# Split weights that start at multiples of 128 bytes, with the x tiles left 32 bytes beyond one, in a float32 decoder layer

## The chip, the cores and the metric

The kernel runs on one core of a Trainium2 chip. The metric is the device time of one execution in microseconds. Three runs of the kernel before gave a median of 1759.82 us (1758.56 to 1761.3). On one core work these engines: TensorE (PE, with its weight loads shown as PEld), VectorE (DVE), ScalarE (ACT), GpSimd (POOL) and SyncE (SP). Each has its own queue of instructions and takes them in order; POOL and SP issue most of the DMAs. Between the engines only semaphores keep order. Operands lie in SBUF, 128 partitions with 229,376 bytes each in the layout of this program; the sums of products lie in PSUM.

## The reference

One layer of a decoder, for 256 rows (S) of 2048 channels (D), in float32:

```python
x = x + 0.5 * swiglu(rmsnorm(x, ffn1_norm[l]), ffn1_w_gate[l], ffn1_w_up[l], ffn1_w_down[l])
h = rmsnorm(x, mix_norm[l])
a_q, a_k, a_v, m_q, m_k, m_v, m_o, m_i, m_f = jnp.split(h @ w_in[l], split_idx, axis=-1)
...
x = x + jnp.concatenate([y_a, y_b], axis=-1) @ w_out[l]
x = x + 0.5 * swiglu(rmsnorm(x, ffn2_norm[l]), ffn2_w_gate[l], ffn2_w_up[l], ffn2_w_down[l])
...
return rmsnorm(x, final_norm)
```

`y_a` is a causal differential attention with 4 heads, `y_b` an mLSTM with 4 heads in chunks of 128 rows. The inner width of each FFN is 5632. Nearly all the arithmetic is in the seven weight matrices of the two FFNs and the two projections, some 50 million weights that are read once.

## The kernel before

**Products.** TensorE multiplies float32r operands. To keep float32 accuracy, each weight and each x is split into a high part (`split`, L132: a cast on ScalarE, `wh` or `xs`/`xt`) and a low part (L133: a subtraction on VectorE, `wl`). `mms` (L177 to L184) then makes three matmuls of each product: L181 high x by high w, L182 low x by high w, L184 high x by low w. The x tile, 128x128, is the stationary operand; the weights, up to 512 columns of float32r, are the moving one. So each 512-column matmul reads 2048 bytes of `wh` or `wl` in every partition.

**Stages.** The kernel runs FFN1, the input projection with the mLSTM gates and the attention beside it, the output projection, and FFN2, in column chunks (`CW` = 512; the q/k part has chunks of 392, 384 and 256). The class `Paired` works two weight matrices or two halves at a time in a scheme that saves products at the price of sums of weights on VectorE (L479, L497) and by accumulating DMAs on POOL (L495, L533); its steps are `leading`, `second_sum` and `sums`. `sums` copies two banks of PSUM to SBUF through ScalarE (`ds` and `us`, L503, called from `sums`) and subtracts them on VectorE (L537, L546). `units` and `plain` do the remaining rows without that scheme.

**Residual and norm.** After a chunk of an FFN or of the output projection, `residual` (or `finish2` for the last FFN, L1211 and L1213) adds it to `xres`, and `square_sum` (L298 to L300) squares the new 512 columns on ScalarE. Only the sum of the squares (`accum_out`) is used; the squares themselves go to a tile called `junk`.

**Order.** The kernel writes no fixed order for the engines: a planner orders each engine's queue when the program is built, by priorities (`tc.high_priority`, with `AHEAD` and `soon`), by when buffers come free, and by a few explicit orders (`after`, `ahead_of_splits`). A tile pool with n buffers gives its tiles out in turn, and a tile waits until the one that held the buffer is done. So a tile that comes from another pool can change the order that the planner finds.

**SBUF.** Pools take their space one behind the other in the order in which they are opened. Before, with the start of the tiles in bytes modulo 128:

| Pool (buffers) | Tiles | First byte | Modulo 128 |
|---|---|---|---|
| const, big | `prm`, `ident` and others; `xres` | 16512; `ident` 16928; `xres` 20256 | `ident` 32; `xres` 32 |
| slots (22) | `xs`, `xt`, 4096 bytes | 36640 | 32 |
| work (8) | ring of 512-column tiles, tag "w" | 126752 | 32, 64, 96, 0 in turn |
| wr (5) | `raw`, 6144 bytes | 143392 | 32 |
| wrp (5) | `rawp`, `late`, 4096 bytes | 174112 | 32 |
| wsp (4 + 4) | `wh` and `wl`, 4096 bytes | 194592 and 210976 | 32 |
| small | sums and scales, `junk` | 227360 | mixed |

The ring tiles of `work` take 2080 bytes each, which is why they rotate. SBUF is full but for 32 bytes. The ring holds `ds`, `us`, `sg`, `xg`, `hg`, `xsum` and `part`, among others.

Of the kernel before, what the change touches and what calls it, by code (L numbers as in the profile page):

```python
# [9 lines left out]
F32 = mybir.dt.float32  # L10
F32R = mybir.dt.float32r
BF16 = mybir.dt.bfloat16
AF = mybir.ActivationFunctionType
# [4 lines left out]
P = 128  # L18
# [6 lines left out]
CW = 512  # L25
# [35 lines left out]
def tile_trunk_layer(ctx: ExitStack, tc: tile.TileContext, x, xt, par, bias_if, lamv, fnorm,  # L61
                     wg1, wu1, wd1, wqk0, wqk1, wqk2, win, wout, wg2, wu2, wd2, out):
    nc = tc.nc
    const = ctx.enter_context(tc.tile_pool(name="const", bufs=1))
    big = ctx.enter_context(tc.tile_pool(name="big", bufs=1))
    slots = ctx.enter_context(tc.tile_pool(name="slots", bufs=22))
    work = ctx.enter_context(tc.tile_pool(name="work", bufs=8))
    wr = ctx.enter_context(tc.tile_pool(name="wr", bufs=5))
    wrp = ctx.enter_context(tc.tile_pool(name="wrp", bufs=5))
    wsp = ctx.enter_context(tc.tile_pool(name="wsp", bufs=4))  # L70
    small = ctx.enter_context(tc.tile_pool(name="small", bufs=2))
    ps_acc = ctx.enter_context(tc.tile_pool(name="ps_acc", bufs=4, space=PSUM))
    ps_tr = ctx.enter_context(tc.tile_pool(name="ps_tr", bufs=2, space=PSUM))

    wqk = [wqk0, wqk1, wqk2]
    uid = [0]

    def nm(s):
        uid[0] += 1
        return f"{s}_{uid[0]}"  # L80


    prm = const.tile([P, N_PAR], F32, name="prm")
    nc.scalar.dma_start(prm, par)
    zeros = work.tile([P, CW], BF16, tag="w", name="zeros")
# [13 lines left out]
        nc.tensor.matmul(seeded(which), zeros[:, 0:P], zeros, start=True, stop=True)  # L99
    for _ in range(WARM):  # L100
        nc.tensor.matmul(warm, zeros[:, 0:P], zeros, start=True, stop=True)
    ident = const.tile([P, P], F32, name="ident")
    nc.gpsimd.memset(ident, 0.0)
    nc.gpsimd.affine_select(out=ident, in_=ident, compare_op=ALU.not_equal, fill=1.0, base=0,
                            pattern=[[-1, P]], channel_multiplier=1)
# [190 lines left out]
        return r  # L296

    def square_sum(src, acc, scale=1.0):  # L298
        j = small.tile([P, CW], BF16, tag="junk", name=nm("junk"), bufs=1)
        nc.scalar.activation(j[:, 0:src.shape[-1]], src, AF.Square, scale=scale, accum_out=acc)  # L300

    def finish_norm(parts):
        tot = small.tile([P, NT], F32, tag="tot", name=nm("tot"))
# [57 lines left out]
    def residual(accs, c, scale, parts):  # L361
        for hb in range(NT):
            add_half(accs[hb], xres[:, hb, c * CW:(c + 1) * CW], scale)
        for hb in range(NT):
            square_sum(xres[:, hb, c * CW:(c + 1) * CW], parts[:, hb, c:c + 1])
# [19 lines left out]
    def wk(name):  # L385
        return work.tile([P, CW], F32, tag="w", name=nm(name))
# [652 lines left out]
    for hb in range(NT):  # L1039
        for h in range(NH):  # L1040
            i = hb * NH + h
            square_sum(hms[hb][:, h, :], ssm[:, i:i + 1], scale=dd[:, i:i + 1])
# [68 lines left out]
    def weighted(h):  # L1111
        ps = ps_acc.tile([P, NT, VD], F32, tag="acc", name=nm("av"))
        vs = [av[h // 2][:, hb, h % 2 * VD:(h % 2 + 1) * VD] for hb in range(NT)]
        nc.tensor.matmul(ps[:, 0, :], wts[h][:, 0:P], vs[0], start=True, stop=True)
        nc.tensor.matmul(ps[:, 1, :], wts[h][:, P:S], vs[0], start=True, stop=False)
        nc.tensor.matmul(ps[:, 1, :], wts[h][:, S:S + P], vs[1], start=False, stop=True)
        ss = small.tile([P, NT], F32, tag="ssa", name=nm("ssa"))
        for hb in range(NT):
            square_sum(ps[:, hb, :], ss[:, hb:hb + 1])
        ra = rsq(ss, NT, float(VD), "ra")  # L1120
        y = mixt([P, NT, VD], name="ya")
        for hb in range(NT):
            vec.tensor_scalar(y[:, hb, :], ps[:, hb, :], ra[:, hb:hb + 1], None, op0=ALU.mult)
        if h == 0:
            side.append(lambda: None)
        side.append(functools.partial(y_transposes, [y[:, hb, :] for hb in range(NT)], 2 * h, gatt))
# [141 lines left out]
```

## Time and profile before

| | |
|---|---|
| Median of three runs | 1759.82 us |
| The profiled execution | 1759.56 us |
| Its span, first to last instruction | 1757.8 us |
| Mean granted TensorE clock | 0.999 |
| HBM read / written | 349.56 MB / 2.10 MB |
| TensorE matmuls in the trace | 7926 |

The profile was taken from one execution. "Busy" counts instructions that do work. A matmul's listed duration runs from its start to the end of its results and overlaps the next ones, so that the rate of matmuls is read from the distance between their starts. In a group of instructions the numbers after the bar are the busy time, the mean duration of one in ns, and the idle time of the engine just before them with what ended it.

### The profile page before, as it was taken

What the parts mean: (1) busy time and instruction counts of PE and PEld (TensorE: products, weight loads), DVE (VectorE), ACT (ScalarE), POOL (GpSimd) and SP (SyncE); (2) the same over time, 40 slices, a digit from 0 to 9 for tenths busy, and PEclk for the clock granted to TensorE, in tenths of its full rate; (3) what the DMA queues carried; (4) which work ended last, traced back from release to release, by engine and by line L of the source; (5) the groups of instructions that cost most, each with busy time, mean ns of one, the idle gap of its engine ahead of it and who ended that gap; (6) DMA issues with size and microseconds to landing.
All of it is one profiled execution on the core that took longest, in us unless ns stands there. A gap on an engine that the chain in (4) does not pass through costs nothing.

```text
span 1757.8 us, 24486 instructions
## 1 busy us (share of the span) xinstructions
PE 1744.6 (99%) x7926; PEld 1437.7 (82%) x7926; DVE 1617.8 (92%) x2189; ACT 1267.4 (72%) x1949; POOL 429.3 (24%) x630
## 2 busy tenths in 40 slices
PE   9999999999999999999999999999999999999998
PEld 7788888888888888987888888888888878888886
DVE  7999999999999999898888999999999999999997
ACT  8666777777677768777687777776777677677765
POOL 0022332322233312012231101122332332233310
PEclk9999999999999999999999999999999999999999
DMA  9787998999799977577886667898998999799973
GB/s 365 251 254 209 259 261 265 253 292 265 218 262 258 263 252 204 185 230 221 236 238 192 209 210 211 260 265 233 258 260 268 241 268 276 232 246 256 283 254 115
DMA packets 155265, 429.72 MB, mean 244 GB/s; under 512 B 17632, under 2 KB 18944, under 8 KB 154880
## 3 DMA queue, kind: packets, MB, share of 16 engines
q0 software_dynamic: 76304, 196.66, 45.1%
q1 hardware_dynamic: 77680, 229.40, 38.0%
q10 hardware_dynamic: 1152, 2.09, 0.3%
q8 instruction: 62, 1.02, 0.2%
q14 instruction: 67, 0.55, 0.1%
HBM read 349.56 MB, written 2.10 MB: 200 GB/s over the span
## 4 chain that ended last, share of the span: by engine, by line
PE 93%; DMA 2%; DVE 2%; issue 1%; ACT 0%; POOL 0%; SPq 0%; POOLq 0%; DVEq 0%; ACTq 0%
PE acc L184 18%; PE acc L181 18%; PE acc L182 18%; PE accn L181 12%; PE accn L182 12%; PE accn L184 12%; DVE wl L133 1%; DMA raw<-in_wg_dram 1%; PE tr L373 1%; DMA raw<-in_wu_dram 1%; PE tr L314 0%; PE sc L1060 0%; DMA rawp<-in_wg_dram 0%; ACT wh L132 0%; PE num L1011 0%
## 5 line engine op out<-in xcount | busy, mean ns | idle before, releaser
L132 ACT CAST wh<-raw 128x512 fp32r<-128x512 f32 (+2 forms) x885 | 601.5, 708 | 214.5 <-PE acc L182 66.3
L133 DVE TENSOR_TENSOR wl<-raw,wh 128x512 fp32r<-128x512 f32 (+2 forms) x885 | 676.1, 793 | 58.4 <-ACT wh L132 54.5
L132 ACT CAST wh<-rawp 128x1024 fp32r<-128x1024 f32 (+3 forms) x308 | 318.2, 1035 | 109.5 <-PE acc L182 55.1
L133 DVE TENSOR_TENSOR wl<-rawp,wh 128x1024 fp32r<-128x1024 f32 (+3 forms) x308 | 367.1, 1197 | 32.0 <-ACT wh L132 29.8
L181 PE MATMUL acc<-wh,xs 128*128 128x512 f32 (+2 forms) x956 | 369.5, 387 | 0.0
L182 PE MATMUL acc<-wh,xs 128*128 128x512 f32 (+2 forms) x956 | 368.9, 386 | 0.0
L184 PE MATMUL acc<-wl,xs 128*128 128x512 f32 (+2 forms) x956 | 317.6, 387 | 0.8 <-DVE wl L133 0.7
L533 POOL DMA_DIRECT2D raw<-late x176 | 152.6, 1053 | 442.7 <-DVE wl L133 422.9
L181 PE MATMUL acc<-wh,xt 128*128 128x512 f32 (+2 forms) x564 | 218.4, 388 | 0.7 <-ACT wh L132 0.7
L182 PE MATMUL acc<-wh,xt 128*128 128x512 f32 (+2 forms) x564 | 217.3, 386 | 0.0
L181 PE MATMUL accn<-wh,xt 128*128 128x512 f32 (+1 forms) x552 | 215.3, 391 | 0.0
L182 PE MATMUL accn<-wh,xt 128*128 128x512 f32 (+1 forms) x552 | 214.7, 390 | 0.0
L479 DVE TENSOR_TENSOR raw<-raw 128x1024 f32<-128x1024 f32 x176 | 211.0, 1217 | 0.8
L184 PEld LDWEIGHTS acc<-wl,xs 128*128 128x128 f32 x956 | 178.3, 188 | 39.2 <-DVE wl L133 3.6
L181 PEld LDWEIGHTS acc<-wh,xs 128*128 128x128 f32 x956 | 179.5, 188 | 36.4 <-ACT wh L132 0.6
L182 PEld LDWEIGHTS acc<-wh,xs 128*128 128x128 f32 x956 | 179.6, 188 | 35.6
L181 PE MATMUL accn<-wh,xs 128*128 128x512 f32 (+1 forms) x408 | 162.6, 400 | 1.9 <-ACT wh L132 1.9
L182 PE MATMUL accn<-wh,xs 128*128 128x512 f32 (+1 forms) x408 | 158.0, 388 | 0.0
L184 PE MATMUL acc<-wl,xt 128*128 128x512 f32 (+2 forms) x564 | 157.6, 386 | 0.0
L495 POOL DMA_DIRECT2D raw<-raw x92 | 78.9, 899 | 322.1 <-DVE wl L133 234.7
L184 PE MATMUL accn<-wl,xt 128*128 128x512 f32 (+1 forms) x552 | 154.7, 388 | 0.0
L184 PE MATMUL accn<-wl,xs 128*128 128x512 f32 (+1 forms) x408 | 140.9, 388 | 0.0
(229 smaller groups left out, 2125.0 us busy)
## 6 DMA issues: line engine op xcount, KB each, us to landing
rawp<-in_wd_dram SPq DMA_DIRECT2D x88, 512.0 KB, 5.6
raw<-late POOLq DMA_DIRECT2D x174, 256.0 KB, 5.3
raw<-in_wu_dram POOLq DMA_DIRECT2D x80, 512.0 KB, 8.4
rawp<-in_wu_dram SPq DMA_DIRECT2D x73, 512.0 KB, 5.1
rawp<-in_wg_dram SPq DMA_DIRECT2D x69, 512.0 KB, 5.2
raw<-raw POOLq DMA_DIRECT2D x92, 256.0 KB, 4.1
raw<-in_wd_dram POOLq DMA_DIRECT2D x44, 512.0 KB, 8.6
late<-in_wg_dram SPq DMA_DIRECT2D x41, 512.0 KB, 9.2
```

The costliest lines, as they stand in the source:

```text
L132: return (nc.scalar.copy(hi, src), nc.vector.tensor_tensor(out=lo, in0=src, in1=hi.bitcast(F32), op=ALU.subtract))
L133: nc.vector.tensor_tensor(out=lo, in0=src, in1=hi.bitcast(F32), op=ALU.subtract))
L181: nc.tensor.matmul(acc, lh, rh, start=first, stop=False, skip_group_check=on)
L182: nc.tensor.matmul(acc, ll, rh, start=False, stop=False, skip_group_check=on)
L184: newest[:] = [nc.tensor.matmul(acc, lh, rl, start=False, stop=last, skip_group_check=on)]
L373: nc.tensor.transpose(tr[:, i, hb * P:(hb + 1) * P], hs[hb][:, k * P:(k + 1) * P], ident)
L479: nc.vector.tensor_tensor(out=raw[:, 0:2, :], in0=raw[:, 0:3:2, :], in1=raw[:, 1:2, :].to_broadcast([P, 2, n]), op=ALU.add)
L495: nc.gpsimd.dma_start(raw[:, 0, :], raw[:, 2, :], accum_op=ALU.add)
L533: nc.gpsimd.dma_start(self.raws[j][:, 0, :], lates[-1][1][:, i, :], accum_op=ALU.add)
```

## The change

The pools are opened in another order: behind `slots` comes a new pool `pad` with one tile of 96 bytes that no instruction uses, then `wsp`, `wrp`, `wr`, and only then `work`. The 96 bytes bring the start of everything behind them from 32 to a multiple of 128, and the sizes of `wsp`, `wrp` and `wr` keep it there. `ident` is now the first tile of its pool and starts at a multiple too. The junk output of `square_sum` goes to a tile of the `work` ring instead of a small bf16 tile of its own.

| Pool | First byte after | Modulo 128 |
|---|---|---|
| const: `ident`, `prm` | 16512, 17024 | 0, 0 |
| slots | 36640 | 32 |
| pad | 126752 | 32 |
| wsp: `wh`, `wl` | 126848, 143232 | 0 |
| wrp | 159616 | 0 |
| wr | 180096 | 0 |
| work | 210816 | 0, 32, 64, 96 in turn |
| small | 227456 | mixed |

The second 392-column slice of a weight tile lies 1568 bytes behind the first: at 64 modulo 128 before, at 32 after.

```diff
     slots = ctx.enter_context(tc.tile_pool(name="slots", bufs=22))
+    pad = ctx.enter_context(tc.tile_pool(name="pad", bufs=1))
+    wsp = ctx.enter_context(tc.tile_pool(name="wsp", bufs=4))
+    wrp = ctx.enter_context(tc.tile_pool(name="wrp", bufs=5))
+    wr = ctx.enter_context(tc.tile_pool(name="wr", bufs=5))
     work = ctx.enter_context(tc.tile_pool(name="work", bufs=8))
-    wr = ctx.enter_context(tc.tile_pool(name="wr", bufs=5))
-    wrp = ctx.enter_context(tc.tile_pool(name="wrp", bufs=5))
-    wsp = ctx.enter_context(tc.tile_pool(name="wsp", bufs=4))
     small = ctx.enter_context(tc.tile_pool(name="small", bufs=2))
...
+    pad.tile([P, 24], F32, name="align")
...
+    ident = const.tile([P, P], F32, name="ident")
     prm = const.tile([P, N_PAR], F32, name="prm")
...
-    ident = const.tile([P, P], F32, name="ident")
...
     def square_sum(src, acc, scale=1.0):
-        j = small.tile([P, CW], BF16, tag="junk", name=nm("junk"), bufs=1)
-        nc.scalar.activation(j[:, 0:src.shape[-1]], src, AF.Square, scale=scale, accum_out=acc)
+        nc.scalar.activation(wk("junk")[:, 0:src.shape[-1]], src, AF.Square, scale=scale, accum_out=acc)
```

Both programs hold the same instructions on every engine; their order differs in 134 of TensorE's 7901 rows, 111 of VectorE's 2191, 99 of ScalarE's 1899, 7 of GpSimd's and 9 of SyncE's. The lines behind the head of the kernel are numbered two higher in the changed file up to `square_sum`, and one higher behind it.

On ScalarE at the end of FFN1, in the last step of a `Paired` chunk (`ds` and `us` are the copies of two PSUM banks, `wh` casts of weights, `junk` the squares), the rows before are:

```order
L503 COPY ds_6255<-acc_6121 128x512
L132 CAST xs_6213<-xg_6210 128x512
L132 CAST wh_6286<-late_6257 128x1024
L132 CAST wh_6296<-late_6273 128x512
L300 ACTIVATE junk_6251,parts_127<-xres 128x512
L132 CAST xs_6220<-xsum_6216 128x512
L132 CAST wh_6303<-raw_6122 128x512
L503 COPY us_6283<-acc_6120 128x512
L132 CAST wh_6303<-raw_6125 128x512
```

The second square comes nine rows behind the first there. After, at the same place:

```order
L134 CAST wh_6290<-late_6261 128x1024
L301 ACTIVATE junk_6255,parts_131<-xres 128x512
L301 ACTIVATE junk_6257,parts_131<-xres 128x512
L504 COPY ds_6259<-acc_6125 128x512
L134 CAST xs_6224<-xsum_6220 128x512
L504 COPY us_6287<-acc_6124 128x512
L134 CAST wh_6300<-late_6277 128x512
L134 CAST wh_6307<-raw_6126 128x512
L134 CAST wh_6307<-raw_6129 128x512
```

Both squares now stand ahead of `ds`, and `ds` and `us` stand on the other side of the casts `wh<-late` that they followed or preceded.

On VectorE at the end of FFN2 (L1211 adds a chunk to `xres`, L1213 multiplies it by the final gain `fn`, L537 subtracts `us`), before:

```order
L1211 SCALAR_TENSOR_TENSOR xres<-accn_3351_16143,xres 128x512
L133 TENSOR_TENSOR wl_16409<-late_16379,wh_16408 128x1024
L1213 TENSOR_TENSOR xres<-xres,fn_16246 128x512
L133 TENSOR_TENSOR wl_16419<-late_16395,wh_16418 128x512
L133 TENSOR_TENSOR wl_16426<-raw_16278,wh_16425 128x512
L133 TENSOR_TENSOR wl_16426<-raw_16281,wh_16425 128x512
L537 TENSOR_TENSOR acc_16277<-acc_16277,us_16405 128x512
L133 TENSOR_TENSOR wl_16438<-raw_16316,wh_16437 128x512
```

And after:

```order
L135 TENSOR_TENSOR wl_16413<-late_16383,wh_16412 128x1024
L1212 SCALAR_TENSOR_TENSOR xres<-accn_3351_16147,xres 128x512
L1212 SCALAR_TENSOR_TENSOR xres<-acc_15986,xres 128x512
L1212 SCALAR_TENSOR_TENSOR xres<-acc_15985,xres 128x512
L1214 TENSOR_TENSOR xres<-xres,fn_16250 128x512 x3
L538 TENSOR_TENSOR acc_16281<-acc_16281,us_16409 128x512
L135 TENSOR_TENSOR wl_16423<-late_16399,wh_16422 128x512
L135 TENSOR_TENSOR wl_16430<-raw_16282,wh_16429 128x512
L135 TENSOR_TENSOR wl_16430<-raw_16285,wh_16429 128x512
L135 TENSOR_TENSOR wl_16442<-raw_16320,wh_16441 128x512
```

Three sums into `xres`, three gains and the subtraction of `us` now stand between the first and the second `wl<-late`, where one gain stood.

## The prediction

> **What bounds the kernel now.** I read the page first, then the busy time by windows, then the groups of matmuls by shape, then single matmuls in the timeline. The page gives the span, the busy shares, the granted clock and the chain of work that ended last:
>
> ```profile
> span 1757.8 us, 24486 instructions
> PE 1744.6 (99%) x7926; PEld 1437.7 (82%) x7926; DVE 1617.8 (92%) x2189; ACT 1267.4 (72%) x1949; POOL 429.3 (24%) x630
> PEclk9999999999999999999999999999999999999999
> PE 93%; DMA 2%; DVE 2%; issue 1%; ACT 0%; POOL 0%; SPq 0%; POOLq 0%; DVEq 0%; ACTq 0%
> ```
>
> TensorE works in 1744.6 of 1757.8 us, at the full clock in every slice, and 93% of the chain is its own. The profiled execution took 1759.56 us, 1.76 us more than its span and within 0.3 us of the median of the runs, 1759.82; the sums below start from 1759.56.
>
> The windows tell whether another engine stands right behind. Columns: window, its length, then busy time with the number of instructions on PE, weight loads, DVE, ACT and POOL, the clock, the share of the DMA engines, GB/s.
>
> ```profile
> 300.00:400.00 100.00, 100.00 (x444) 81.94 (x443) 94.70 (x119) 73.79 (x108) 32.72 (x47) 1.00 0.93 263
> 400.00:500.00 100.00, 100.00 (x450) 82.61 (x450) 94.99 (x120) 71.17 (x103) 26.59 (x40) 1.00 0.87 251
> ...
> 600.00:700.00 100.00, 100.00 (x465) 83.16 (x464) 97.10 (x136) 77.17 (x126) 20.15 (x33) 1.00 0.77 235
> ...
> 1100.00:1200.00 100.00, 100.00 (x450) 82.56 (x449) 96.17 (x126) 74.52 (x111) 23.50 (x31) 1.00 0.89 252
> ...
> 1300.00:1400.00 100.00, 100.00 (x446) 81.61 (x445) 94.49 (x121) 73.28 (x107) 29.46 (x43) 1.00 0.89 245
> 1400.00:1500.00 100.00, 99.41 (x443) 81.05 (x443) 94.32 (x122) 69.75 (x103) 29.43 (x44) 1.00 0.91 278
> ...
> 1600.00:1700.00 100.00, 99.83 (x448) 81.84 (x447) 97.21 (x128) 74.83 (x111) 30.00 (x43) 1.00 0.88 246
> ```
>
> TensorE is full in all of them, and VectorE, which makes the low halves of the weights, is 94 to 97% busy in seven of seventeen. So TensorE sets the time, and the question is what one matmul costs. Nearly all of them have 512 columns; these are the four groups of the hi·hi product:
>
> ```profile
> L181 PE MATMUL acc<-wh,xs 128*128 128x512 f32 x914 | 356.8, 390 | 0.0
> ...
> L181 PE MATMUL accn<-wh,xt 128*128 128x512 f32 x540 | 211.5, 392 | 0.0
> L181 PE MATMUL acc<-wh,xt 128*128 128x512 f32 x540 | 211.2, 391 | 0.7 <-ACT wh L132 0.7
> ...
> L181 PE MATMUL accn<-wh,xs 128*128 128x512 f32 x392 | 157.0, 402 | 1.9 <-ACT wh L132 1.9
> ```
>
> They are 914 + 540 + 540 + 392 = 2386 matmuls, and L182 and L184 have as many each: **7158**. The 390 ns of one are a latency; what counts is the distance between starts. In the timeline (start, duration), for 512, 392, 384 and 256 columns:
>
> ```profile
> 402.32 0.39 PE L181 MATMUL acc<-wh,xt 128*128 128x512 f32 x1
> 402.55 0.39 PE L182 MATMUL acc<-wh,xt 128*128 128x512 f32 x1
> ...
> 403.91 0.39 PE L182 MATMUL acc<-wh,xt 128*128 128x512 f32 x1
> ```
>
> ```profile
> 696.40 0.34 PE L181 MATMUL acc<-wh,xs 128*128 128x392 f32 x1
> ...
> 698.01 0.34 PE L182 MATMUL accn<-wh,xs 128*128 128x392 f32 x1
> ```
>
> ```profile
> 717.17 0.33 PE L181 MATMUL acc<-wh,xs 128*128 128x384 f32 x1
> ...
> 719.08 0.33 PE L182 MATMUL acc<-wh,xs 128*128 128x384 f32 x1
> ```
>
> ```profile
> 730.04 0.28 PE L181 MATMUL acc<-wh,xs 128*128 128x256 f32 x1
> ...
> 731.00 0.28 PE L184 MATMUL acc<-wl,xs 128*128 128x256 f32 x1
> ```
>
> 512 columns: 7 steps in 1.59 us, 227 ns. 392: 9 steps in 1.61 us, 178.9 ns. 384: 11 steps in 1.91 us, 173.6 ns. 256: 8 steps in 0.96 us, 120 ns. From 256 to 384 to 512 each 128 columns add 53.5 ns, 0.417 ns a column. So 512 columns should take 213.5 ns, 384 should take 160.2, 256 should take 106.8: **each matmul has 13.3 ns on top, whatever its length**. That is the time of 32 columns, or 128 bytes of a float32 row.
>
> **The change, part by part.** It adds no instruction and removes none.
>
> *Where the weights start.* All weight tiles (wh, wl, and the raw tiles they are made from) start at 32 bytes past a multiple of 128 before, and at a multiple after; the x tiles stay at 32. The moving operand of 512 columns is 2048 bytes a partition, which is 16 pieces of 128 bytes if it starts at a multiple, and touches 17 if it does not. If TensorE reads such pieces whole, the 17th costs just 13.3 ns, and 13 and 9 pieces instead of 12 and 8 give the 384 and 256 column rows too. So the trace allows that the surcharge is the misaligned start. It allows equally that it is a fixed price of changing the stationary tile. The 392 columns decide as far as the trace can: from 32 or from 64 their 1568 bytes touch 13 pieces, as 384 columns do, so pieces alone give 173.4 ns; a fixed 13.3 ns gives 392 × 0.417 + 13.3 = 176.8. Measured is 178.9. The fixed price is the nearer, 2.1 ns off against 5.5. I take it: **0 us** from the start of the tiles on TensorE. The other end is 13.3 ns × 7158 = 95 us less; the lower side, dearer matmuls, is a rival below.
>
> The Trainium skill, "SBUF — State Buffer", section "Door 1: The DMA port swizzle", says that SBUF has 16-byte cachelines and that a read pays when it crosses to a new one; by it a start at 32 is on a line already and the change gives TensorE nothing. No row here shows such a line. The Trainium skill, "TensorE: Matmul & The Clock Gate", section "Wait — 56ns, not 53.3ns?", speaks against that zero: a warm 512-column matmul should follow the one before after 215.7 ns. This trace has 227; if the difference of 11.3 ns went, the sum would be an estimated 81 us lower.
>
> *VectorE and ScalarE* read and write those weights as well. Here operands at different starts can be compared:
>
> ```profile
> L133 DVE TENSOR_TENSOR wl<-raw,wh 128x512 fp32r<-128x512 f32 x698 | 456.2, 686 | 49.1 <-ACT wh L132 45.4 <-PE acc L184 2.7
> ...
> L133 DVE TENSOR_TENSOR xs<-xsum,xs 128x512 fp32r<-128x512 f32 x40 | 27.3, 686 | 1.4 <-ACT xs L132 1.4
> ```
>
> The weights' subtraction has all operands at 32; `xsum` comes from the rotating work ring and stands at 32, 64, 96 or 0. Both take 686 ns: cost 0.
>
> *The squares' output.* `square_sum` writes its unused result to a slot of the work ring as float32 instead of a bf16 tile of its own.
>
> ```profile
> L300 ACT ACTIVATE junk<-xres 128x512 bf16<-128x512 f32 x22 | 13.9, 630 | 2.7 <-DVE xres L1211 2.5
> ...
> L132 ACT CAST xs<-xg 128x512 fp32r<-128x512 f32 x13 | 8.0, 627 | 0.2
> ...
> L300 ACT ACTIVATION_READ_ACCUMULATOR junk<-xres 128x1 f32 x26 | 4.9, 189 | 0.0
> ```
>
> A cast of the same size that writes four bytes an element takes 627 ns against the square's 630, so the wider write itself is 0. But a square now takes a turn in the ring of eight, and the planner has put squares ahead of the `ds` and `us` copies and of weight casts in four places: the ends of FFN1, of the 392-column part, of the output projection and of FFN2. In the first three two squares go ahead, 0.63 + 0.19 = 0.82 us each. Queued behind them on ScalarE stand `ds`, `us` and the `wh` casts, for which VectorE (the subtractions) and then TensorE wait. At the end of FFN2 VectorE also runs three residual sums and three gains in front of the `us` subtraction and of `wl<-late`, where before it ran one gain:
>
> ```profile
> 1721.65 1.22 DVE L133 TENSOR_TENSOR wl<-late,wh 128x1024 fp32r<-128x1024 f32 x1
> 1722.79 0.68 DVE L1213 TENSOR_TENSOR xres<-xres,fn 128x512 f32<-128x512 f32 x1
> 1723.39 0.68 DVE L133 TENSOR_TENSOR wl<-late,wh 128x512 fp32r<-128x512 f32 x1
> ```
>
> From start to start such a step takes 0.60 us (1722.79 to 1723.39); six more in front (the sums, the gains and the subtraction are seven against one) make 3.6 us that `wl` comes later. What covers all this is the lead of the splits: the quoted rows blame ScalarE for only 1.9 + 0.7 us of idle TensorE in the whole run. At best that vanishes (−2.6 us). At worst nothing covers: three places × 2 × 0.82, and 3.6 + 3 × 0.82 at the fourth, 11.0 us. I take one uncovered square at three of the four places, near the row that shows almost no idle: 3 × 0.82 = **2.5 us**. The few DMA issues that change places among themselves on SP and POOL I cost at 0, since they are prefetches; without that cover one late load of 5 us could show, which the range holds.
>
> *The identity matrix* goes from 32 to a multiple. It is the moving operand of the transposes, of which this is the largest group:
>
> ```profile
> L373 PE MATMUL tr<-ident,sg 128*128 128x128 f32 x176 | 24.2, 273 | 0.0
> ```
>
> A 13.3 ns saved or lost on each would be 2.3 us here and twice that for all transposes; I take 0, as for the weights.
>
> Sum: 1759.56 + 0 + 2.5 = **1762**, own range 1755 to 1771.
>
> **The rivals.**
>
> *The surcharge is the start (fast).* For it: 13.3 ns is just 128 bytes' worth at three lengths. Against it: the 392 columns. Price: 95 us, and 3.8 us for the 282 shorter matmuls, less what VectorE then holds back. TensorE would need 213.7/227 = 0.941 of each window; VectorE has more than that in the seven quoted windows, by 0.6, 0.9, 3.0, 2.1, 0.4, 0.2 and 3.1 us, together 10.3. So 1759.6 − 99 + 10.3 = 1671, and some 4 us more for order and waits: **1675**, between 1668 and 1690. Half the surcharge, if only one of two pieces at the ends goes, would give 1712.
>
> *Weights and x at different starts disturb one another (slow).* Before, weights and x are both at 32; after, the moving operand at 0 and the stationary tile at 32 are read at once. The 392-column rows are the only ones in which the two differ (weights at 32 or 64), and they cost 178.9 − 176.8 = 2.1 ns too much. On all 7158 that is 15 us: 1777. A second row bounds it from above, matmuls that follow a wait near the start, at the full clock:
>
> ```profile
> 8.04 0.40 PE L182 MATMUL accn<-wh,xs 128*128 128x512 f32 x1
> 8.28 0.39 PE L181 MATMUL accn<-wh,xs 128*128 128x512 f32 x1
> 8.51 0.39 PE L182 MATMUL accn<-wh,xs 128*128 128x512 f32 x1
> ```
>
> Two steps in 0.47 us, 235 ns; 8 ns on all of them would be 57 us, 1817. I take **1777**. It decides as soon as a 512-column step is above 227.5 ns (0.5 × 7158 = 3.6 us). Against it: a stationary tile is loaded beside the matmul, 82% of the time already, without showing.
>
> *The layout might not come out as described.* The addresses in the built programs do change as told, so this has no weight of its own; its time would be that of the first case.
>
> **How the numbers follow.** Chances: no effect of the start 0.52, fast 0.34, slow 0.14. A measurement of this kernel can tell about 0.2%, 3.5 us, from no change. The first case falls within that with 0.31, above with 0.16, below with 0.05. So faster 0.34 + 0.05 = 0.39, same 0.31, slower 0.16 + 0.14 = 0.30. The predicted time is that of the likeliest case, 1762. The range reaches down into the fast case, to 1670, and up to 1773, which takes in the bound of the order's cost; the dear end of the slow case and the lowest of the fast stay outside, some 0.18.
>
> **What would show it.** The step between 512-column matmuls: 227 ns means I am right on the start, 213 to 216 the fast rival, 228 to 235 the slow one. With 227, idle TensorE blamed on `wh` casts and `wl` near 670, 705, 1010 and 1725 us should grow by some 2.5 us, and the 392-column step tells whether its 2.1 ns hang on the start. In the fast case VectorE should be 97 to 100% busy and the waits of TensorE for `wl` should lead the chain in those windows. I would be wrong if the step changed, or if the prefetched loads slipped so that single waits of 5 to 10 us for DMA came or went.

## The result and the profile after

The changed kernel takes **1803.77 us** (median of 4 runs, 1803.11 to 1804.39), the kernel before, measured beside it, 1759.47 us (1758.56 to 1761.3). The ratio is put at 1.0247, with a 95% interval from 1.0234 to 1.0259. It is slower by 44 us.

The page after, with the lines that answer to those of before:

```profile
span 1802.6 us, 24479 instructions
PE 1789.3 (99%) x7926; PEld 1441.8 (80%) x7926; DVE 1624.7 (90%) x2189; ACT 1270.2 (70%) x1949; POOL 428.1 (24%) x630
PEclk9999999999999999999999999999999999999999
PE 96%; issue 1%; DMA 1%; DVE 1%; ACT 1%; POOL 0%; POOLq 0%; SPq 0%; DVEq 0%; ACTq 0%
```

The span is 44.8 us longer, and TensorE is busy for 44.7 us more with the same 7926 matmuls, at nearly the same mean granted clock (0.998 against 0.999). Its share of the chain went from 93 to 96%. No wait was added in bulk: the matmuls themselves are slower.

The windows after (columns as before) say so stretch by stretch:

```profile
300.00:400.00 100.00, 99.99 (x433) 79.83 (x432) 92.80 (x117) 70.52 (x104) 33.51 (x48) 1.00 0.93 257
400.00:500.00 100.00, 100.00 (x439) 80.46 (x438) 92.86 (x118) 69.36 (x101) 23.95 (x35) 1.00 0.84 241
...
600.00:700.00 100.00, 100.00 (x447) 80.41 (x446) 94.78 (x127) 75.83 (x118) 24.12 (x38) 1.00 0.77 221
...
1100.00:1200.00 100.00, 100.00 (x439) 80.47 (x438) 93.58 (x123) 74.76 (x114) 21.42 (x26) 1.00 0.90 246
```

Between 400 and 500 us TensorE is full as before, yet it does 439 matmuls where it did 450. VectorE has become less busy. In the timeline of TensorE after (start, duration) the steps can be read one by one:

```profile
402.30 0.39 PE L183 MATMUL accn<-wh,xt 128*128 128x512 f32 x1
402.53 0.39 PE L184 MATMUL accn<-wh,xt 128*128 128x512 f32 x1
402.76 0.40 PE L183 MATMUL accn<-wh,xt 128*128 128x512 f32 x1
403.00 0.39 PE L184 MATMUL accn<-wh,xt 128*128 128x512 f32 x1
...
405.10 0.39 PE L183 MATMUL acc<-wh,xs 128*128 128x512 f32 x1
```

There are 12 steps in the 2.80 us from 402.30 to 405.10, 233.3 ns instead of 227. They come in threes of 231, 232 and 237 ns. Over all pairs of neighbouring 512-column matmuls (some 7,070), without the steps above 245 ns, in which something was waited for, the mean is **233.41 ns after and 227.14 before**.

The other engines show nothing of the new starts. These groups after are the subtraction that makes `wl`, the cast that makes `wh`, the square and the largest group of transposes:

```profile
L135 DVE TENSOR_TENSOR wl<-raw,wh 128x512 fp32r<-128x512 f32 x698 | 455.1, 684 | 57.9 <-ACT wh L134 44.2 <-PE acc L186 10.9 <-issue 1.0
...
L134 ACT CAST wh<-raw 128x512 fp32r<-128x512 f32 x698 | 408.6, 620 | 204.2 <-PE acc L184 72.3 <-PE accn L184 34.2 <-DVE raw L480 33.1
...
L301 ACT ACTIVATE junk<-xres 128x512 f32<-128x512 f32 x22 | 13.8, 628 | 7.9 <-DVE xres L1212 4.1 <-DVE xres L360 3.8
...
L374 PE MATMUL tr<-ident,sg 128*128 128x128 f32 x176 | 24.1, 272 | 0.0
```

The subtraction takes 684 ns against 686, the cast 620 against 622, the square that now writes float32 628 against 630, and the transposes 272 against 273.

### The profile page after: what moved, and what is told of

Same layout as the page of the kernel before. It is cut to its first block, busy times and chain, and to the rows that moved or that the text cites. A ratio compares the mean times of both kernels' runs of the same rounds, so it can differ in the third digit from the quotient of the medians.

```text
span 1802.6 us, 24479 instructions
## 1 busy us (share of the span) xinstructions
PE 1789.3 (99%) x7926; PEld 1441.8 (80%) x7926; DVE 1624.7 (90%) x2189; ACT 1270.2 (70%) x1949; POOL 428.1 (24%) x630
## 4 chain that ended last, share of the span: by engine, by line
PE 96%; issue 1%; DMA 1%; DVE 1%; ACT 1%; POOL 0%; POOLq 0%; SPq 0%; DVEq 0%; ACTq 0%
PE acc L186 19%; PE acc L183 19%; PE acc L184 19%; PE accn L183 12%; PE accn L184 12%; PE accn L186 12%; PE tr L374 1%; DMA raw<-in_wg_dram 1%; DVE wl L135 1%; PE sc L1061 0%; PE tr L315 0%; DMA raw<-raw 0%; PE num L1012 0%; ACT wh L134 0%; PE tr L1100 0%
## 5 line engine op out<-in xcount | busy, mean ns | idle before, releaser
L183 PE MATMUL acc<-wh,xs 128*128 128x512 f32 (+2 forms) x956 | 375.1, 393 | 0.8 <-ACT us L504 0.8
L184 PE MATMUL acc<-wh,xs 128*128 128x512 f32 (+2 forms) x956 | 374.4, 392 | 0.0
L186 PE MATMUL acc<-wl,xs 128*128 128x512 f32 (+2 forms) x956 | 323.4, 393 | 0.1
L183 PE MATMUL acc<-wh,xt 128*128 128x512 f32 (+2 forms) x564 | 221.3, 393 | 0.7 <-ACT wh L134 0.7
L184 PE MATMUL acc<-wh,xt 128*128 128x512 f32 (+2 forms) x564 | 220.4, 391 | 0.0
L184 PE MATMUL accn<-wh,xt 128*128 128x512 f32 (+1 forms) x552 | 217.7, 394 | 0.0
L183 PE MATMUL accn<-wh,xt 128*128 128x512 f32 (+1 forms) x552 | 217.6, 394 | 0.0
L183 PE MATMUL accn<-wh,xs 128*128 128x512 f32 (+1 forms) x408 | 165.6, 407 | 0.8 <-ACT wh L134 0.6
L184 PE MATMUL accn<-wh,xs 128*128 128x512 f32 (+1 forms) x408 | 161.2, 396 | 0.0
```

Of the source, the lines that this page charges most:

```text
L183: nc.tensor.matmul(acc, lh, rh, start=first, stop=False, skip_group_check=on)
L184: nc.tensor.matmul(acc, ll, rh, start=False, stop=False, skip_group_check=on)
L186: newest[:] = [nc.tensor.matmul(acc, lh, rl, start=False, stop=last, skip_group_check=on)]
```

## The experiments

The question was why a step is dearer, and what part of the 44 us is the order. In all the layer's kernels below every engine runs the rows of the changed kernel in its order; only the places in SBUF differ, by the size or the position of the filler, except in `ring_only`, which keeps the layout of before.

**w32_order_kept**: weights back at 32 modulo 128.

```diff
-    pad.tile([P, 24], F32, name="align")
+    pad.tile([P, 32], F32, name="align")
```

> The changed kernel with a filler of 128 bytes instead of 96: wh, wl and raw start at 32 modulo 128 again, as x does; every engine runs the same rows in the same order as in the changed kernel. Theory A (the step of a matmul depends on where the weights start relative to x): the 512-column step goes back from 233.3 to 226.7 ns, 6.67 ns x 7158 = 48 us less than 1803.8, so about 1757 to 1762. Theory B (the moved squares and the new order cost the time): stays at 1800 to 1806.

It took 1797.95 us, a ratio of 1.0214 (1.0198 to 1.0230). Its window, and a piece of its timeline:

```profile
400.00:500.00 100.00, 100.00 (x440) 80.90 (x439) 92.90 (x117) 69.91 (x102) 24.37 (x35) 1.00 0.85 241
```

```profile
402.51 0.40 PE L183 MATMUL accn<-wh,xt 128*128 128x512 f32 x1
402.74 0.40 PE L184 MATMUL accn<-wh,xt 128*128 128x512 f32 x1
402.98 0.40 PE L183 MATMUL accn<-wh,xt 128*128 128x512 f32 x1
403.22 0.39 PE L184 MATMUL accn<-wh,xt 128*128 128x512 f32 x1
```

Theory A fell in the form in which I had it: weights and x both start at 32 modulo 128 as before, and the steps are still 228 to 241 ns (mean of all below 245 ns: 232.63), 440 matmuls in the window. The time alone comes within some 2 us of the range of theory B, the order. What speaks against B is that these matmuls wait for nothing and are longer all the same; the runs below settle it, since `w0_x0`, `filler_256` and `ring_only` have this very order and steps of 227.15 to 227.17 ns.

**w0_x0**: the filler ahead of the x tiles, so that weights and x both start at multiples of 128.

```diff
+    pad = ctx.enter_context(tc.tile_pool(name="pad", bufs=1))
     slots = ctx.enter_context(tc.tile_pool(name="slots", bufs=22))
-    pad = ctx.enter_context(tc.tile_pool(name="pad", bufs=1))
```

> The changed kernel with its filler ahead of the x tiles: weights and x both start at multiples of 128 bytes, the same rows in the same order. Theory A (only the distance between the starts counts): 226.7 ns a step, 1757 to 1762. Theory C (a moving operand that starts at a multiple of 128 is dearer by itself): 233.3 ns, 1800 to 1806. Theory D (each operand that starts off a multiple costs a piece of its own): below 226.7 ns, down to 213.3, then VectorE holds the time near 1675 to 1700.

It took 1764.61 us, a ratio of 1.0020 (1.0008 to 1.0033), with the fast step:

```profile
400.00:500.00 100.00, 100.00 (x450) 82.61 (x450) 95.55 (x121) 71.68 (x105) 27.10 (x41) 1.00 0.88 252
```

450 matmuls in the window, as before. The step is the one that theory A named; the time is 2.6 us above its range of 1757 to 1762, which had left nothing for the order (see `ring_only`). So a moving operand at a multiple of 128 is not dearer (theory C), and two aligned operands are not cheaper (theory D): the 13.3 ns on top are not a 17th piece of 128 bytes.

**map_of_starts**: matmuls alone, in one execution; the layer is left out. `w` and `s` are the starts of the moving and the stationary operand.

```python
for c, (dt, n, size, w, s) in enumerate(CASES):
    ...
    nc.tensor.matmul(acc[:, 0:n], xt[:, h, o:o + P], wt[:, t, w:w + n],
                     start=first, stop=last)
```

> A kernel of matmuls alone, which leaves the layer out and copies x to the output: 48 matmuls in a row for each pair of starts of the moving and the stationary operand (0, 32, 64, 96 modulo 128 each, and some finer ones), for 512, 384, 256 and 128 columns in float32r, and for bf16. Theory A: the step depends on the difference of the starts alone: 226.7 ns on the diagonal, 233.3 where the moving one is 32 below (0 and 32, 32 and 64, 64 and 96, 96 and 0). Theory C: it depends on the moving one's start alone. Theory D: it is smallest, 213.3, at 0 and 0. If the interference needs float32r at full rate, bf16 shows one step for all pairs.

A row of its timeline joins the matmuls in the window asked for. Three cases, with the moving operand at 0 and x at 32, both at 32, and 96 with 32:

```profile
24.38 10.19 PE L51 MATMUL acc<-ws,xs 128*128 128x512 f32 x43
```

```profile
69.20 10.36 PE L51 MATMUL acc<-ws,xs 128*128 128x512 f32 x45
```

```profile
157.96 10.24 PE L51 MATMUL acc<-ws,xs 128*128 128x512 f32 x44
```

Less 0.39 us for the last one's own length, these are 9.80 us in 42 steps, 233.3 ns; 9.97 in 44, 226.6; 9.85 in 43, 229.1. Steps in ns for 512 columns in float32r, from the starts in the trace, mean of the last 36 of 48 (0 and 0 was the first case and began with steps of 427 ns; its last steps are 226 and 227):

| moving at | x at 0 | x at 32 | x at 64 | x at 96 |
|---|---|---|---|---|
| 0 | 226.7 | 233.3 | 233.3 | 234.4 |
| 32 | 233.3 | 226.7 | 233.3 | 233.3 |
| 64 | 228.9 | 233.3 | 226.7 | 233.3 |
| 96 | 233.3 | 228.9 | 233.3 | 226.7 |

Only the difference of the starts counts on this grid, and nothing is below 226.7. In bf16 all four pairs tried (0 and 32) take 215.8 ns, so the effect shows with float32r operands and not with these. In float32r the same four pairs all give 173.3 ns for 384 columns; for 256, equal starts are even the dearer ones (120.0 against 118.3 and 116.7); and 128 columns take 111.7 ns at all four.

In this map the tiles lie a multiple of 256 bytes apart (5120). In the layer before the distance from the x tiles to `wh` is 194592 − 36640 = 157952, 617 × 256; in `w0_x0` it is 352 × 256; in the changed kernel 352 × 256 + 96; and in `w32_order_kept` 352 × 256 + 128. That gave the next theory: the distance counts modulo 256, not 128.

**filler_256** and **filler_64** test it in the layer: 64 and 16 elements of four bytes in the filler instead of 24.

```diff
-    pad.tile([P, 24], F32, name="align")
+    pad.tile([P, 64], F32, name="align")
```

> The changed kernel with a filler of 256 bytes: weights and x both at 32 modulo 128, as with the filler of 128 bytes, but the distance from the x tiles to the weights is now a multiple of 256 bytes (90368) instead of an odd multiple of 128 (90240). The same rows in the same order. Theory E (the step is 226.7 ns only where the distance is a multiple of 256 bytes): 226.7 ns, 1762 to 1767 as the kernel with both at 0. Theory F (what counts is the starts modulo 128, and the slow step of the 128-byte filler comes from where wsp lies now): about 234 ns again, 1796 to 1800.

> The changed kernel with a filler of 64 bytes: weights at 96, x at 32 modulo 128, distance 64 modulo 256. The same rows in the same order. The map of starts gives 228.9 ns for 96 and 32. Theory E and the map: 228.9 ns a step, (228.9 - 226.7) x 7158 = 16 us above the kernel with both at 0, so about 1780 (1775 to 1784). Theory F or a two-valued step: 233.3 ns, 1798 to 1806.

`filler_256` took 1764.49 us, 1.0026 (1.0014 to 1.0039); `filler_64` 1775.22 us, 1.0089 (1.0074 to 1.0104). The window of each:

```profile
400.00:500.00 100.00, 100.00 (x451) 82.62 (x450) 94.96 (x120) 70.71 (x103) 27.05 (x40) 1.00 0.87 250
```

```profile
400.00:500.00 100.00, 100.00 (x447) 81.92 (x446) 94.24 (x118) 70.06 (x101) 26.58 (x39) 1.00 0.84 241
```

The filler of 256 and that of 128 bytes have the same starts modulo 128 and the same order. With 256 the window holds 451 matmuls, with 128 it holds 440. Theory E stands, theory F is out. A distance of 64 gives the step between, 229.08 ns, as the map had it, and a time in the range given for it, though nearer its low end.

**map_of_distance**: the finer map, with stationary tiles of fewer columns too.

> Matmuls alone again, the layer left out: 32 in a row of 512 columns in float32r, x at a multiple of 256 bytes, weights at every 32 bytes over 544 bytes beyond it; then some starts off the 32-byte grid; then stationary tiles of 128, 96, 64 and 32 columns. Theory E: 226.7 ns at distances 0, 256 and 512 only, some 233 at most others, 128 among them (the layer with the 128-byte filler had about 234). If the 13.3 ns are the reads of the stationary tile that get in between those of the moving one, the step falls in proportion to the stationary columns: 223.3, 220.0 and 216.7 ns for 96, 64 and 32. If they are a fixed price of changing it, 226.7 for all.

Distances of 128 and of 256 bytes:

```profile
51.13 7.39 PE L46 MATMUL acc<-ws,xs 128*128 128x512 f32 x31
```

```profile
80.78 7.21 PE L46 MATMUL acc<-ws,xs 128*128 128x512 f32 x31
```

With 0.39 us off, 30 steps take 7.00 and 6.82 us, 233.3 and 227.3 ns. Over 31 steps of each case:

| distance | 0 | 32 | 64 | 96 | 128 | 160 | 192 | 224 | 256 | 288 | 320 | 512 |
|---|---|---|---|---|---|---|---|---|---|---|---|---|
| ns | 226.7 | 233.4 | 229.2 | 233.7 | 233.5 | 234.1 | 233.4 | 233.1 | 227.5 | 233.4 | 229.2 | 227.5 |

The row repeats after 256 bytes, as theory E has it; where 256 and 512 show 227.5, the first steps after the case before were longer, and the rest are 226 and 227. Off the 32-byte grid no simple rule is left: a distance of 252 gives 226.7, but 232.4 in `map_of_starts`, where weights at 0 and x at 4 have the same distance modulo 256; 260 gives 236.6; and with both operands at 8 or at 24 beyond a multiple of 256, distance 0, the step is 233.4 and 233.7.

The second half failed both of its expectations. At distances of 0 and 128 bytes, 96 stationary columns give 230.1 and 226.7 ns, 64 give 230.1 and 229.4, and 32 give 231.4 and 230.7. The surcharge neither falls with the columns nor stays at 13.3 ns; with 96 columns, 384 bytes, the better of the two distances is 128 and no longer 0. The second half also repeats one case of the first, 128 columns at a distance of 128 bytes: it took 233.5 ns in the first half, with steps of 229 and 238 in turn, and 232.3 in the second, in another pattern.

**map_high_low**: the two stationary tiles, or the two moving ones, at different starts.

> Matmuls alone, the layer left out: 32 in a row of 512 columns in float32r, now with the two stationary tiles that take turns (the high and the low x) at different starts, and with the two moving tiles at different starts. If each matmul's step follows from the distance of its own two operands (theory E as it stands), a pair with one tile at a distance of 0 and the other at 32 gives the mean of 226.7 and 233.3, 230.0, and nothing falls below 226.7. If instead the state is carried over from one matmul to the next, some mixed pairs give 226.7 or less, or 233.3 in full. A mixed pair below 226 would be a layout for the layer that beats both kernels: 1 ns less is 7 us.

No pair is below 226.7, so this gave no layout to try in the layer. The pair of x tiles at 0 and 32 takes 234.7 ns, more than either of them alone (226.7 and 233.1), where the mean of the two, 229.9, was expected; the pair at 0 and 64 takes 229.7, close to its mean. So a step does not follow from its own two operands alone: something is carried over from one matmul to the next. The case that `map_of_distance` has twice, at 233.5 and 232.3 ns, says the same.

**ring_only**: the kernel before, with the squares in the work ring.

```diff
-        j = small.tile([P, CW], BF16, tag="junk", name=nm("junk"), bufs=1)
-        nc.scalar.activation(j[:, 0:src.shape[-1]], src, AF.Square, scale=scale, accum_out=acc)
+        nc.scalar.activation(wk("junk")[:, 0:src.shape[-1]], src, AF.Square, scale=scale, accum_out=acc)
```

> The kernel before with one part of the change alone: the squares go to the work ring. Starts of all tiles as before, every engine's rows in the order of the changed kernel. If the order costs what the prediction took: 226.7 ns a step and 1762 (1759.5 to 1768). If the order is more than that of the lost time: above 1770.

It took 1766.19 us against 1760.75 for the kernel before, measured beside it, 1.0033 (1.0019 to 1.0046): 5.4 us, with the fast step of 227.17 ns. The other two kernels with this order and the fast step, `w0_x0` and `filler_256`, lie 5.2 and 3.7 us above theirs. Where these microseconds arise is seen by the start of the same matmul in both traces. These are the delays in us against the kernel before, first at a place in its time:

| us in the kernel before | ring_only | filler_256 | changed kernel |
|---|---|---|---|
| 652.0 | 0.0 | 0.7 | 16.6 |
| 702.3 | 3.0 | 3.3 | 20.9 |
| 1035.3 | 2.9 | 3.2 | 26.9 |
| 1088.0 | 4.1 | 4.4 | 28.7 |
| 1275.1 | 4.0 | 4.3 | 33.7 |
| 1302.3 | 6.0 | 4.3 | 34.5 |
| 1706.7 | 6.0 | 3.1 | 43.2 |
| 1748.9 | 6.8 | 3.9 | 44.9 |

With the fast step the delay comes in jumps: 3 us at the passage from FFN1 to the 392-column part, 1.1 in the output projection, 0.8 at the end of FFN2. The 2.0 us near 1300 are not in `filler_256`, which has the same order, so they are not the order's. In the changed kernel the delay grows all along the run, by some 2 to 2.7 us in each 100, and the first jump sits on top of it.

The first jump in the timeline of ScalarE in `ring_only`:

```profile
698.53 1.28 ACT L772 ACT_TABLE_LOAD   x1
699.83 0.20 ACT L772 ACTIVATE lexp<-lsum 128x2 f32<-128x2 f32 x1
699.94 0.62 ACT L299 ACTIVATE junk<-xres 128x512 f32<-128x512 f32 x1
700.46 0.19 ACT L299 ACTIVATION_READ_ACCUMULATOR junk<-xres 128x1 f32 x1
700.55 0.62 ACT L299 ACTIVATE junk<-xres 128x512 f32<-128x512 f32 x1
701.08 0.19 ACT L299 ACTIVATION_READ_ACCUMULATOR junk<-xres 128x1 f32 x1
701.17 0.46 ACT L502 COPY ds<-acc 128x392 f32<-128x392 f32 x1
701.54 0.48 ACT L502 COPY us<-acc 128x392 f32<-128x392 f32 x1
```

And TensorE there, with the idle time before each and what ended it:

```profile
700.30 0.62 PE L184 MATMUL accn<-wl,xs 128*128 128x392 f32 x2 [1.60 <-DVE wl L133]
702.07 0.44 PE L181 MATMUL acc<-wh,xs 128*128 128x392 f32 x1 [0.71 <-ACT us L502]
704.47 0.45 PE L184 MATMUL accn<-wl,xs 128*128 128x392 f32 x1 [0.35 <-DVE wl L133]
```

The largest wait, 1.60 us, is for a `wl` of VectorE. The timeline of VectorE in `ring_only` says why that `wl` is late:

```profile
698.01 0.43 DVE L768 TENSOR_TENSOR lv<-lv 128x256 f32<-128x256 f32 x1 [2.21 <-DMA lv<-in_lamv_dram]
...
699.28 0.97 DVE L133 TENSOR_TENSOR wl<-late,wh 128x784 fp32r<-128x784 f32 x1
```

VectorE stands still for 2.21 us, until the load of `lv`, a parameter of the attention, has landed, and only then makes `wl`. In the kernel before, the same product came late enough to find `lv` there. Its place, and those of `us`, of the first square and of the table load, were:

```profile
701.17 0.42 DVE L769 TENSOR_TENSOR lv<-lv 128x256 f32<-128x256 f32 x1
```

```profile
697.66 0.49 ACT L503 COPY us<-acc 128x392 f32<-128x392 f32 x1
...
698.80 0.63 ACT L300 ACTIVATE junk<-xres 128x512 bf16<-128x512 f32 x1
...
704.55 1.28 ACT L773 ACT_TABLE_LOAD   x1
```

So the two squares and the table load, which ran behind these copies before, now stand ahead of `ds` and `us`, and cost TensorE the 0.71 us in which it waits for `us`. More of the jump, 1.60 us, comes from VectorE's new order, in which `lv` stands ahead of `wl`. The changed kernel shows the same two waits, 1.28 and 0.80 us, behind a wait of VectorE of 2.12 us for `lv`.

## Why the prediction was wrong

I forecast 1762 us, with a range up to 1773, and gave the case that came about a chance of 0.14.

*The step that failed* is "0 us from the start of the tiles on TensorE". In its place the runs show 233.41 − 227.14 = 6.27 ns a matmul, on 7158 of them 44.9 us. My reasoning weighed two causes of the 13.3 ns on top of a matmul, a 17th piece or a fixed price, and took "not the 17th piece" for "the start does not matter". The first half was right: in `w0_x0`, with both operands at multiples of 128, the mean step is 227.15 ns. The second half did not follow from it. The fixed price does not hold either, since 13.3 ns on top of 128 columns would be 66.7 ns, and the map has 111.7. And the 392-column rows, which decided between the two, could not tell: their step is 178.9 to 179.2 ns in all seven kernels of the layer (steps with a wait left out), whatever the distance.

*The slow rival* was right in its mechanism as far as the runs show it, that the step depends on how the two operands lie to each other, and in the point from which it decides, a step above 227.5 ns. Its size was wrong: it took 2.1 ns from the 392-column rows and gave 1777 us. Its bound from the steps after a wait, 8 ns, was nearer to the 6.27 measured, and those very steps were the sign that I passed over: after a wait the kernel before shows steps such as 236, 228, 232 and 231 ns and then settles at 227, with operands at the same distance, so that 227 was not a fixed price but a state that holds under conditions. The rival also had the condition wrong. Not the starts modulo 128 count, as `w32_order_kept` shows, but, for starts on the 32-byte grid, the distance modulo 256.

*The fast rival* (1675 us, chance 0.34) was out: no layout of the layer and no case of the maps at 512 columns in float32r has a mean step below 226.7 ns. The rule of the Trainium skill, "TensorE: Matmul & The Clock Gate", section "Wait — 56ns, not 53.3ns?", of 215.7 ns holds here for bf16, where the map gives 215.8; float32r does not reach it at any start tried.

*The 16-byte lines* of the Trainium skill, "SBUF — State Buffer", section "Door 1: The DMA port swizzle", led to the same zero as my sum, and the measurements decide against it: starts that all lie on such lines differ by some 7 ns a matmul.

*The order* was forecast at 2.5 us, between −2.6 and 11.0. The three kernels with this order and the fast step are 3.7 to 5.4 us above the kernel before: the sign was right, and the forecast half to two thirds of it. The mechanism was right in part. I had spread the cost over squares at three of four places; more than half of it sits at one, near 700 us, where the squares and the table load explain 0.71 us of idle TensorE. The 1.60 us there come from VectorE waiting for the load of `lv`, a wait that my sum did not have. Near 670 us, where I expected a part, the delay does not grow.

*VectorE, ScalarE, the transposes and the wider write of the square* at 0: right, by the rows of after.

*The sum*: 44.9 + 5.4 = 50.3 us, and 44.3 were measured. Steps above 245 ns, less 226.7 each, add up to 14.3 us before, 18.5 in `ring_only` and 12.5 in the changed kernel, so the changed kernel has 6.0 us of waits less than `ring_only`, which brings the sum to 44.3. I read this as VectorE and the loads being in time more often when TensorE is slower; no run tests it by itself. That the figures meet to a tenth is luck: the order's 5.4 us could as well be 3.7, and the changed kernel's trace has a stretch in which the granted clock fell after the waits for `lv` and `us`, to 0.86 over 10 us (the third figure from the end), which the sum leaves out and which is an estimated 1.4 us (0.14 × 10):

```profile
720.00:730.00 10.00, 10.00 (x51) 9.96 (x51) 9.18 (x14) 7.79 (x14) 2.92 (x5) 0.86 0.63 201
```

## What to carry to other kernels

When TensorE is full, read the step between matmuls, not only busy shares: 450 or 439 matmuls in the same full 100 us were the whole of this change. In float32r with 512 columns and 128x128 stationary tiles, the distance in SBUF between the moving and the stationary operand should be a multiple of 256 bytes, with both starts on the 32-byte grid; here pools that are opened in another order, or a filler, decide over some 2% of the time without a single instruction changed. And if a trace shows two values for the same step, look for the condition that picks one before calling either a fixed price.

## What the runs showed of the hardware

- With 128x128 stationary tiles and both starts on the 32-byte grid, a float32r matmul of 512 columns steps at 226.7 ns if the distance between its operands is a multiple of 256 bytes, at some 229 ns at 64 bytes beyond one, and at 232 to 234 ns at the other multiples of 32. The longer steps repeat in patterns (231, 232, 237 at 96 bytes; 229, 238 at 128). At 128 bytes the mean is 233.5 or 232.3 in the same map, and 232.6 in the layer.
- bf16 matmuls of 512 columns step at 215.8 ns at each of four pairs of starts, 128 columns at 55.8.
- At 256 columns in float32r unequal starts are the faster ones: 116.7 and 118.3 ns against 120.0. At 128 columns the step is 111.7 ns at all four pairs. At 384 columns it is 173.3 ns in the map, and in the layer 173.4 to 173.7 ns at distances of 0 and 64 bytes and 176.0 and 176.6 at 128 and 96.
- What is left open: what repeats every 256 bytes, why at 512 columns even the best distance costs 13.3 ns on top of the columns, why fewer stationary columns do not lower the step and, at 96, move the good distance, and what a matmul carries over to the next. That the reads of the two operands collide is a guess that would fit; no run here showed it.
